# Seven-product down projection: when two activation sums are formed, where four result sums are kept, and how many pages the weight stream may use

## The chip, the cores and the metric

The kernel runs on one core of a Trainium2 chip. The metric is device time in microseconds, from a launch to its end. Its engines run side by side, each through its own queue in order: TensorE (PE, with its weight loads as PEld), VectorE (DVE), ScalarE (ACT), GpSimd (POOL), and SyncE (SP), which here only issues DMAs.

## What is computed

A two-layer decoder trunk over 256 tokens of width 2048, in float32. Each layer is a token mixer with an output projection, then a gated feed-forward block; each of the two adds a normed result to the stream x. The change lies in the feed-forward block and in the helpers it shares:

```
def swiglu(u, w_gu, w_down):
    gu = u @ w_gu                                            # (256, 2048) @ (2048, 2*5632)
    return (jax.nn.silu(gu[..., :D_FF]) * gu[..., D_FF:]) @ w_down   # (256, 5632) @ (5632, 2048)
x = x + rmsnorm(swiglu(rmsnorm(x, g[2]), ...), g[3])
```

## The kernel before, in words

**Products.** Float32 accuracy comes from splitting each operand into a rounded part and a remainder (hi, lo) and adding three matmuls: hi·hi, lo·hi, hi·lo. Activations are split once; weights are streamed and split as they come.

**Pages.** SBUF is cut into 44 pages of 4 KB per partition (`NPAGE`, class `Pages`), handed out first freed, first used. A page may be handed out while the engines still have to read it in the order of the queues; the new writer then waits for that reader.

**The weight stream.** `_unit_list` writes down the order of all weight units (128x1024, 512 KB). `dma_one` loads one into a page (a raw unit); `split_one` makes hi on ScalarE (L231) and lo on VectorE (L232), two pages, and gives the raw page back. `take` (L270 on) is called once for each unit: it returns the unit's parts and, before that, works ahead: twice it loads until 3 raw units are held and splits one further unit, then it loads a fourth raw unit (L284). `room(n)` lets it do so only while n pages beyond `st["res"]` (the reserve) are free; `st["look"]` bounds how many units ahead may be split. With no page to spare a unit is split only at its own `take`. `give` hands the two pages back behind the unit's last matmul.

**Side work.** Evacuations, norms and sums are generators; `tick`, called between matmul groups, advances one of them by one step, and a yielded number is the count of ticks to its next step. So side work is queued on ScalarE and VectorE between splits, in the order of the calls.

**Feed-forward.** `ffn` first runs the gate-up stage: 22 groups of 256 columns, each of 8 units (L928, `x_unit`, matmuls at L398 to L400). `gu_evac` turns a group into the transposed activations `hT` (one page per group, 22 in all), and for the last 8 groups (`DN_S`, 14 to 21) also into four sums of 128x128 blocks, `sp` (one page each, `s_parts`, L878, read from PSUM). The normed input `xf` takes 8 pages, released when the last `hT` page is claimed.

**Down projection.** `pair(cp)` runs twice, for the first and the last 1024 columns. For 14 of the 22 row groups it multiplies plainly (`x_step`: units of kind a and b, 12 matmuls each at L954 to L956). For the other 8 it uses a seven-product scheme on 2x2 blocks (`quad`: 4 takes named a, b, T13 and T24, 21 matmuls of 128x512; VectorE forms weight differences at L247, L248, L257 and L258). `_dn_steps` lays the kinds out: in pair 0 four a steps first, in pair 1 three, then the S steps woven among the others, and b steps last. All eight PSUM banks hold P1 to P7 and Q. After the last S step `sums` forms four combined sums in two pages of their own (`ut`, L988). `block` (L1004) then adds one result bank to its sum (VectorE, L1007), and `Tail.rows` squares it on ScalarE for the norm (L633) and multiplies it by the norm's gain row into a page `og` (VectorE, L639). The four blocks of pair 0 are queued while pair 1 runs its second unit. The gain rows `gb` come by a broadcast DMA from POOL's queue, which also carries the `xraw` loads of the next stage. In pair 1 each step frees one `hT` page and an S step also its `sp` page; x is read back into 4 pages, and layer 0 fills 8 pages `mT` and claims 8 pages `kT` for what follows, `mem_k`. The last four b units are taken together (`last_units`).

Of the kernel before, what the change touches and what calls it, by code (L numbers as in the profile page):

```python
# [10 lines left out]
F32 = mybir.dt.float32  # L11
F32R = mybir.dt.float32r
BF16 = mybir.dt.bfloat16
AF = mybir.ActivationFunctionType
OP = mybir.AluOpType
AX = mybir.AxisListType

P = 128
S = 256
D = 2048  # L20
KT = D // P
HD = 128
DFF = 5632
FT = DFF // P
# [69 lines left out]

DN_S = tuple(range(14, FT // 2))


def _dn_steps(cp):  # L100
# [93 lines left out]
def trunk(ctx: ExitStack, tc: tile.TileContext, a: dict, out: bass.AP):  # L194
    nc = tc.nc
    sb = ctx.enter_context(tc.tile_pool(name="sb", bufs=1))
    tmp = ctx.enter_context(tc.tile_pool(name="tmp", bufs=1))
# [9 lines left out]
    raws, parts = {}, {}  # L207
# [59 lines left out]
    def room(n):  # L267
        return len(pages.own) + len(pages.free) >= st["res"] + n

    def take(name):  # L270

        i = st["i"]
        assert units[i][0] == name, (units[i], name)
        while st["dma"] <= i:
            dma_one()
        while st["split"] <= i:
            split_one()
        n = len(units)
        for _ in range(0 if st["quiet"] else 2):
            while st["dma"] < n and len(raws) < NRAW and room(1):  # L280
                dma_one()
            if st["split"] < min(i + 1 + st["look"], n, st["dma"] - 1 if st["dma"] < n else n) and room(2):
                split_one()
        while not st["quiet"] and st["dma"] < n and len(raws) < 4 and room(1):  # L284
            dma_one()
        st["i"] += 1
        return parts.pop(i)
# [9 lines left out]
    def spawn(g):  # L297
        side.append([g, clock["t"]])
# [28 lines left out]
    def need(X, kts):  # L327
        until(lambda: X.done.issuperset(kts))
# [73 lines left out]
    def x_unit(pts, name, X, kt0, w, first, last, free=False):  # L402

        u = take(name)
        for k in range(2):
            need(X, (kt0 + k,))
            for t in range(2):
                x_mm(pts[t][1], u, X, kt0 + k, k, t, w, first and k == 0, last and k == 1)
                tick()
                tick()  # L410
        give(u)
        if free:
            X.drop()
# [203 lines left out]
    class Tail:  # L617
# [14 lines left out]
        def rows(self, c, t, src, pre=None):  # L632
            nc.scalar.activation(junk[:, :512], src, AF.Square, accum_out=self.ssq[:, t, c:c + 1])  # L633
            if pre is not None:
                rstd_of(pre, self.ssq[:, t, c:c + 1], t, self.r)
            hs, pg = slice((c % 2) * 512, (c % 2 + 1) * 512), 2 * t + c // 2
            if pg not in self.og:
                self.og[pg] = pages.get([P, 1024], F32, "og")
            nc.vector.tensor_tensor(out=self.og[pg][1][:, hs], in0=src, in1=self.gb[c // 2][1][:, hs], op=OP.mult)  # L639
            if c == 1 and t == 1:  # L640
                pages.put(self.gb.pop(0)[0])

        def chunk(self, c, pts, ts=(0, 1), pre=None):
            self.gain((c + 1) // 2 if c < 3 else 1)
            for t in ts:
                self.rows(c, t, pts[t][1], pre)
                banks.put(pts[t][0])
# [227 lines left out]
    free_mem(0)  # L875


    def s_parts(A):  # L878

        sv = tmp.tile([P, 4, P], F32, tag="sv", name="sv")  # L880
        sp = pages.get([P, 4, 2, P], F32R, "sp")
        tt = nc.vector.tensor_tensor
        s1 = tmp.tile([P, P], F32, tag="s11", name="s11")
        nc.scalar.activation(s1, A[:, 0, 1], AF.Copy)
        tt(out=sv[:, 0], in0=A[:, 1, 1], in1=s1, op=OP.add)
        tt(out=sv[:, 1], in0=sv[:, 0], in1=A[:, 0, 0], op=OP.subtract)
        tt(out=sv[:, 2], in0=A[:, 0, 0], in1=s1, op=OP.subtract)
        tt(out=sv[:, 3], in0=A[:, 1, 0], in1=sv[:, 1], op=OP.subtract)
        yield 1
        nc.scalar.activation(sp[1][:, :, 0, :], sv, AF.Copy)  # L890
        nc.vector.tensor_tensor(out=sp[1][:, :, 1, :], in0=sv, in1=sp[1][:, :, 0, :].bitcast(F32), op=OP.subtract)
        return sp

    def gu_evac(f2, pts, H, rf, Sp):

        while "r" not in rf:
            yield 0
        H.grow()
        hs = []
        for t in range(2):  # L900
            r = rf["r"][:, t:t + 1]
            g = tmp.tile([P, S], F32, tag="ev1", name="ev1", bufs=2)
            nc.scalar.activation(g, pts[t][1][:, :S], AF.Silu, scale=r)  # L903
            h = tmp.tile([P, S], F32, tag="ev2", name="ev2", bufs=2)
            nc.vector.scalar_tensor_tensor(h, pts[t][1][:, S:], r, g, op0=OP.mult, op1=OP.mult)  # L905
            banks.put(pts[t][0])
            hs.append(h)
        yield 8
        (b, p), = yield from sbank()
        for k in range(2):  # L910
            for t in range(2):
                nc.tensor.transpose(p[:, k * S + t * P:k * S + (t + 1) * P], hs[t][:, k * P:(k + 1) * P], ident)
        pv = p.rearrange("p (k q) -> p k q", k=2)
        hp = H.t[f2][1]
        yield 2
        nc.scalar.activation(hp[:, :, 0, :], pv, AF.Copy)
        nc.vector.tensor_tensor(out=hp[:, :, 1, :], in0=pv, in1=hp[:, :, 0, :].bitcast(F32), op=OP.subtract)
        if f2 in DN_S:
            Sp[f2] = yield from s_parts(p.rearrange("p (k t q) -> p k t q", k=2, t=2))
        banks.put(b)  # L920
        H.done.update((2 * f2, 2 * f2 + 1))

    def ffn(l, X, rf, gidx, step=lambda u: None, first=lambda c: None):
        H, Sp = XT(pages, 0, "hT"), {}
        st["res"] = 2
        for fs in [(0, 1)] + [(f2,) for f2 in range(2, FT // 2)]:
            pts = [[bank(), bank()] for _ in fs]
            for u in range(KT // 2):  # L928
                for p in pts:
                    x_unit(p, f"gu{l}", X, 2 * u, 512, u == 0, u == KT // 2 - 1)  # L930
            for f2, p in zip(fs, pts):
                spawn(gu_evac(f2, p, H, rf, Sp))
        until(lambda: len(H.t) == FT // 2)
        X.release()
        st["res"] = 3
        tail = Tail(gidx, "f")
        steps = 0

        def pair(cp):
            bk, n, T = {}, {}, {}  # L940
# [44 lines left out]
            def sums():  # L985

                yield 12
                tp = [pages.get([P, 2, 512], F32, "ut") for _ in range(2)]  # L988
                s1, u2, u3, v = (tp[j // 2][1][:, j % 2, :] for j in range(4))
                T["pages"], T["left"] = tp, 4  # L990
                tt = nc.vector.tensor_tensor
                nc.scalar.activation(s1, bk["P1"][1], AF.Copy)
                free("P1")
                tt(out=u2, in0=bk["P6"][1], in1=s1, op=OP.add)
                free("P6")
                tt(out=u3, in0=bk["P7"][1], in1=u2, op=OP.add)
                free("P7")
                yield 2
                tt(out=v, in0=bk["P5"][1], in1=u3, op=OP.add)
                tt(out=u2, in0=bk["P5"][1], in1=u2, op=OP.add)  # L1000
                free("P5")
                T["c"] = {"P2": (0, 0, s1), "P3": (1, 0, u2), "P4": (0, 1, u3), "Q": (1, 1, v)}

            def block(key, pre=None):  # L1004

                c, t, s_ = T["c"][key]
                nc.vector.tensor_tensor(out=s_, in0=bk[key][1], in1=s_, op=OP.add)  # L1007
                free(key)
                tail.rows(2 * cp + c, t, s_, pre)
                T["left"] -= 1  # L1010
                if not T["left"]:
                    for e in T["pages"]:
                        pages.put(e[0])

            def blocks_of(keys):
                yield 8
# [43 lines left out]
            body = plan if cp == 0 else plan[:-HOLD]  # L1060
            for j, (kd, u) in enumerate(body):
                if kd == "S":
                    need(H, (2 * u, 2 * u + 1))
                    until(lambda: u in Sp)
                    quad(u)
                    if cp == 1:
                        pages.put(Sp.pop(u)[0])
                        H.drop_one(u)
                else:
                    x_step(kd, u)  # L1070
                    if cp == 1 and kd == "b":
                        H.drop_one(u)
                if cp == 1 and kd in "Sb":
                    on_step()
                left = [e[0] for e in plan[j + 1:]]
                if "S" not in left and kd == "S":
                    spawn(sums())
                if "a" not in left and "S" not in left and (kd == "a" or kd == "S") and cp == 1:
                    spawn(blocks_of(("P2", "P4")))
            if cp == 0:  # L1080
                tail.gain(1)
                spawn(blocks_of(("P2", "P3", "P4", "Q")))
            else:
                last_units(plan[-HOLD:])
# [2 lines left out]
        pair(1)  # L1087
        tail.finish()
        H.release()
        return tail  # L1090

    Xf = XT(pages, KT, "xf")
# [409 lines left out]
```

## Time and profile before

| | |
|---|---|
| median of 3 runs | 2570.41 us (2570.28 to 2574.23) |
| the profiled execution | 2570.08 us, its span 2568.3 us |
| DVE, ACT, POOL busy | 1623.4, 1257.5, 59.9 us |
| DMA | 491.26 MB, mean 191 GB/s |
| layer 0: gate-up ends, pair 1 starts, down projection ends | about 1123, 1242 and 1364 us |
| layer 1: the same | about 2325, 2442 and 2558 us |

The span runs from the first to the last instruction. A matmul lasts longer in the records than the distance to the next one, since they are pipelined; so the pace is read from starts, or from how many matmuls a stretch holds. "Idle" is the time an engine had nothing running before an instruction, put down to what came last.

### The profile page before, as it was taken

The numbers are of one execution on the slowest core, as the hardware profiler recorded it, in microseconds if no ns is written. First come the engines' busy times: TensorE is split into PE (matmuls) and PEld (weight loads), VectorE is DVE, ScalarE is ACT, GpSimd is POOL, SyncE is SP. The second block draws the span as 40 slices with busy tenths as digits, with TensorE's granted clock in tenths as the row PEclk, the third lists the DMA queues.
The fourth block names the chain that finished last, engine by engine and source line by source line (L and its number), as shares of the span: only waits on it lengthen the run. The fifth ranks groups of instructions, "written<-read, shape, count | busy, mean of one in ns | idle before, by whom it ended". The sixth has DMA issues, their size and how long they took to land. (4 is left out here: it accounts for less than half of the span.)

```text
span 2568.3 us, 32470 instructions
## 1 busy us (share of the span) xinstructions
PE 2512.2 (98%) x12230; PEld 2121.7 (83%) x12230; DVE 1623.4 (63%) x2230; ACT 1257.5 (49%) x1804; POOL 59.9 (2%) x73
## 2 busy tenths in 40 slices
PE   8999999999999999999999999999899999999998
PEld 6899999988888888878787888888788888877876
DVE  8564555567544455568797766796644555547796
ACT  7444444456433344444565566565543444445553
POOL 5000000000000000000000000000000000000000
PEclk9999999999999999999999999999999999999999
DMA  8455555576555555556575676346655555546664
GB/s 304 147 182 170 170 161 177 173 256 245 188 185 184 181 180 167 162 180 209 190 271 203 213 243 212 115 140 222 202 175 182 182 183 174 165 148 213 205 217 176
DMA packets 138318, 491.26 MB, mean 191 GB/s; under 512 B 15664, under 2 KB 15664, under 8 KB 138160
## 3 DMA queue, kind: packets, MB, share of 16 engines
q1 hardware_dynamic: 134208, 477.06, 57.0%
q0 software_dynamic: 3232, 11.01, 1.3%
q8 instruction: 96, 1.57, 0.3%
q10 hardware_dynamic: 720, 1.11, 0.1%
q14 instruction: 62, 0.51, 0.1%
HBM read 482.82 MB, written 6.29 MB: 190 GB/s over the span
## 5 line engine op out<-in xcount | busy, mean ns | idle before, releaser
L232 DVE TENSOR_TENSOR lo<-raw,hi 128x1024 fp32r<-128x1024 f32 (+2 forms) x899 | 1048.7, 1205 | 360.7 <-ACT hi L231 327.9
L231 ACT ACTIVATE hi<-raw 128x1024 fp32r<-128x1024 f32 (+2 forms) x899 | 891.7, 1036 | 237.3 <-PE bk L400 131.6
L398 PE MATMUL bk<-hi,xf 128*128 128x512 f32 x1408 | 554.9, 394 | 5.3 <-ACT hi L231 4.7
L400 PE MATMUL bk<-lo,xf 128*128 128x512 f32 x1408 | 550.4, 391 | 1.5 <-DVE lo L232 1.4
L399 PE MATMUL bk<-hi,xf 128*128 128x512 f32 x1408 | 549.4, 390 | 0.0
L363 PE MATMUL bk<-xT,hi 128*128 128x512 f32 x1104 | 398.7, 404 | 0.0
L398 PEld LDWEIGHTS bk<-hi,xf 128*128 128x128 f32 x1408 | 265.6, 189 | 59.5 <-ACT hi L231 5.6
L400 PEld LDWEIGHTS bk<-lo,xf 128*128 128x128 f32 x1408 | 265.3, 188 | 59.2 <-DVE lo L232 3.5
L399 PEld LDWEIGHTS bk<-hi,xf 128*128 128x128 f32 x1408 | 265.7, 189 | 53.7 <-DVE xf L452 0.2
L365 PE MATMUL bk<-xT,lo 128*128 128x256 f32 x1035 | 289.5, 280 | 0.0
L363 PEld LDWEIGHTS bk<-xT,hi 128*128 128x128 f32 x1104 | 204.0, 188 | 39.8 <-issue 0.2
L954 PE MATMUL bk<-hi,hT 128*128 128x512 f32 x544 | 213.5, 392 | 6.4 <-ACT hi L231 6.4
L956 PE MATMUL bk<-lo,hT 128*128 128x512 f32 x544 | 213.6, 393 | 2.4 <-DVE lo L232 2.4
L955 PE MATMUL bk<-hi,hT 128*128 128x512 f32 x544 | 212.7, 391 | 0.0
L365 PEld LDWEIGHTS bk<-xT,lo 128*128 128x128 f32 x1035 | 195.4, 189 | 3.1
L905 DVE SCALAR_TENSOR_TENSOR ev<-bk,r_f,ev 128x256 f32<-128x256 f32 x88 | 42.2, 484 | 202.1 <-ACT ev L903 193.1
L903 ACT ACTIVATE ev<-bk,r_f 128x256 f32<-128x256 f32 x88 | 41.5, 474 | 227.4 <-PE bk L400 226.3
L954 PEld LDWEIGHTS bk<-hi,hT 128*128 128x128 f32 x544 | 103.0, 189 | 29.2 <-ACT hi L231 8.1
L956 PEld LDWEIGHTS bk<-lo,hT 128*128 128x128 f32 x544 | 102.8, 189 | 25.9 <-DVE lo L232 4.6
L955 PEld LDWEIGHTS bk<-hi,hT 128*128 128x128 f32 x544 | 102.8, 189 | 21.3
L390 ACT ACTIVATE ev<-bk 128x256 f32<-128x256 f32 x93 | 35.6, 383 | 129.5 <-PE bk L363 129.5
L391 DVE TENSOR_TENSOR ev<-bk,ev 128x256 f32<-128x256 f32 x93 | 39.3, 423 | 91.5 <-ACT ev L390 90.8
(246 smaller groups left out, 3037.6 us busy)
## 6 DMA issues: line engine op xcount, KB each, us to landing
raw<-in_gu SPq DMA_DIRECT2D x352, 512.0 KB, 3.6
raw<-in_dn SPq DMA_DIRECT2D x176, 512.0 KB, 4.4
raw<-in_a_qk SPq DMA_DIRECT2D x96, 512.0 KB, 3.8
raw<-in_a_v SPq DMA_DIRECT2D x64, 384.0 KB, 3.1
raw<-in_cw SPq DMA_DIRECT2D x32, 512.0 KB, 4.6
raw<-in_b_out SPq DMA_DIRECT2D x32, 512.0 KB, 4.2
raw<-in_a_out SPq DMA_DIRECT2D x24, 512.0 KB, 4.4
raw<-in_b_q SPq DMA_DIRECT2D x24, 512.0 KB, 3.9
```

Source lines behind the costliest of these rows:

```text
L231: nc.scalar.activation(hi, src, AF.Copy)
L232: nc.vector.tensor_tensor(out=lo, in0=src, in1=hi.bitcast(F32), op=OP.subtract)
L363: mm(pt[:, :], lhsT=hi[:, ks], rhs=X.hl(kt), start=first, stop=last)
L365: mm(pt[:, S:], lhsT=lo[:, ks], rhs=X.part(kt, 0), start=False, stop=False)
L398: mm(p[:, :w], lhsT=xh, rhs=u[0][1][:, ws], start=f, stop=False)
L399: mm(p[:, :w], lhsT=xl, rhs=u[0][1][:, ws], start=False, stop=False)
L400: mm(p[:, :w], lhsT=xh, rhs=u[1][1][:, ws], start=False, stop=l)
L903: nc.scalar.activation(g, pts[t][1][:, :S], AF.Silu, scale=r)
L905: nc.vector.scalar_tensor_tensor(h, pts[t][1][:, S:], r, g, op0=OP.mult, op1=OP.mult)
L954: mm(p, lhsT=xh, rhs=wh, start=f, stop=False)
L955: mm(p, lhsT=xl, rhs=wh, start=False, stop=False)
L956: mm(p, lhsT=xh, rhs=wl, start=False, stop=e)
```

## The change

- The same 8 row groups take the seven-product scheme, in another order: 14, 15, 16, 17, 20, 21, 18, 19. For 18 and 19 (`DN_LATE`) the block sums are no longer formed in the gate-up stage. A new generator `s_late`, queued as the down projection starts, adds hi and lo of `hT` back together into a page `hw` (VectorE, 128x512) and forms the sums from there.
- `take` loads the fourth raw unit only with three pages to spare (`room(3)`).
- In the last gate-up group `x_unit` gives back one page of `xf` after each unit.
- `sums` writes its four sums into the halves of the `og` pages, waiting until two pages are free, and `Tail.rows` multiplies them there in place. The `ut` pages are gone.
- The second gain row is loaded when the first is given back.
- The reserve in the down projection is 2 or 0 by step, where it was 3; the bound of units split ahead is 6 there.

```
-DN_S = tuple(range(14, FT // 2))
+DN_S = (14, 15, 16, 17, 20, 21, 18, 19)
+DN_LATE = (18, 19)
...
-        while not st["quiet"] and st["dma"] < n and len(raws) < 4 and room(1):
+        while not st["quiet"] and st["dma"] < n and len(raws) < 4 and room(3):
...
             if c == 1 and t == 1:
                 pages.put(self.gb.pop(0)[0])
+                self.gain(1)
...
-            self.gain((c + 1) // 2 if c < 3 else 1)
...
+    def s_late(H, Sp):
+
+        for u in DN_LATE:
+            h = H.t[u][1].bitcast(F32)
+            i, w = pages.get([P, 2, S], F32, "hw")
+            nc.vector.tensor_tensor(out=w, in0=h[:, :, 0, :], in1=h[:, :, 1, :], op=OP.add)
+            A = w.rearrange("p k (t q) -> p k t q", t=2)
+            Sp[u] = yield from s_parts(A, A[:, 0, 1])
+            pages.put(i)
+            yield 16
...
-        if f2 in DN_S:
-            Sp[f2] = yield from s_parts(p.rearrange("p (k t q) -> p k t q", k=2, t=2))
+        if f2 in DN_S and f2 not in DN_LATE:
+            Sp[f2] = yield from s_psum(p)
...
-                    x_unit(p, f"gu{l}", X, 2 * u, 512, u == 0, u == KT // 2 - 1)
+                    x_unit(p, f"gu{l}", X, 2 * u, 512, u == 0, u == KT // 2 - 1, fs[0] == FT // 2 - 1)
...
-        st["res"] = 3
...
+        spawn(s_late(H, Sp))
...
                 yield 12
-                tp = [pages.get([P, 2, 512], F32, "ut") for _ in range(2)]
-                s1, u2, u3, v = (tp[j // 2][1][:, j % 2, :] for j in range(4))
-                T["pages"], T["left"] = tp, 4
+                while len(pages.free) + len(pages.own) < 2:
+                    yield 0
+                for t in range(2):
+                    tail.og[2 * t + cp] = pages.get([P, 1024], F32, "og")
+                st["res"] = 0
+                s1, u2, u3, v = (tail.og[2 * (j // 2) + cp][1][:, j % 2 * 512:(j % 2 + 1) * 512] for j in range(4))
...
                 if kd == "S":
+                    st["res"], st["look"] = 0 if j > 8 or cp else 2, 6
...
                 if "S" not in left and kd == "S":
+                    st["res"] = 2 if cp == 0 else 0
                     spawn(sums())
...
             if cp == 0:
-                tail.gain(1)
                 spawn(blocks_of(("P2", "P3", "P4", "Q")))
...
         H.release()
+        st["look"] = 4
```

## Rows read from the trace of the kernel before

**Rows 1.** The page, part 1: busy time of each engine over the span.
```profile
PE 2512.2 (98%) x12230; PEld 2121.7 (83%) x12230; DVE 1623.4 (63%) x2230; ACT 1257.5 (49%) x1804; POOL 59.9 (2%) x73
```

**Rows 2.** Waits of PE, whole span: who <- for whom: us, times, longest.
```profile
PE bk L398 <- ACT hi L231: 10.7, 3, 6.0
...
PE bk L954 <- ACT hi L231: 6.7, 5, 2.9
```

**Rows 3.** Waits of PE, layer 0, 1094 to 1128 us.
```profile
PE bk L398 <- ACT hi L231: 2.4, 1, 2.4
PE bk L954 <- ACT hi L231: 1.5, 1, 1.5
PE bk L400 <- DVE lo L232: 0.5, 1, 0.5
PE bk L956 <- DVE lo L232: 0.5, 1, 0.5
```

**Rows 4.** Timeline of PE, layer 1: start, us, instruction, [idle before].
```profile
2306.21 0.73 PE L398 MATMUL bk<-hi,xf 128*128 128x512 f32 x1 [2.37 <-ACT hi L231]
...
2326.20 0.50 PE L954 MATMUL bk<-hi,hT 128*128 128x512 f32 x1 [1.51 <-ACT hi L231]
...
2327.46 0.50 PE L956 MATMUL bk<-lo,hT 128*128 128x512 f32 x1 [0.52 <-DVE lo L232]
```

**Rows 5.** Stretches: length; busy and count of PE, PEld, DVE, ACT, POOL; PEclk; DMA.
```profile
1094.00:1112.00 18.00, 15.10 (x62) 11.75 (x61) 8.23 (x12) 5.62 (x9) 0.00 (x0) 0.91 0.33 114
1120.00:1132.00 12.00, 9.96 (x39) 7.51 (x38) 6.55 (x8) 5.72 (x8) 0.58 (x1) 0.86 0.84 309
1160.00:1200.00 40.00, 40.00 (x178) 32.73 (x177) 32.62 (x38) 19.99 (x22) 0.00 (x0) 1.00 0.65 211
1246.00:1258.00 12.00, 8.55 (x29) 6.24 (x28) 7.20 (x9) 5.43 (x10) 0.00 (x0) 0.86 0.42 124
...
1290.00:1330.00 40.00, 40.00 (x178) 33.14 (x177) 39.54 (x48) 26.44 (x34) 2.14 (x4) 1.00 0.80 261
...
1366.00:1380.00 14.00, 12.70 (x67) 11.03 (x68) 10.96 (x16) 7.26 (x11) 0.80 (x1) 0.88 0.86 336
...
2300.00:2312.00 12.00, 9.53 (x36) 6.96 (x36) 4.81 (x8) 4.29 (x6) 0.00 (x0) 0.86 0.21 65
2322.00:2332.00 10.00, 7.97 (x36) 5.96 (x36) 6.79 (x8) 6.29 (x8) 0.48 (x1) 1.00 0.86 297
```

**Rows 6.** The page, part 6: loads of down-projection units, median us to landing.
```profile
raw<-in_dn SPq DMA_DIRECT2D x176, 512.0 KB, 4.4
```

**Rows 7.** Waits of PE, layer 0, 1364 to 1372 us.
```profile
PE bk L363 <- ACT hi L231: 2.5, 1, 2.5
PE bk L365 <- DVE lo L232: 0.8, 1, 0.8
```

**Rows 8.** Waits of PE, layer 0, 1246 to 1268 us.
```profile
PE bk L954 <- ACT hi L231: 3.2, 2, 2.9
PE bk L956 <- DVE lo L232: 1.5, 3, 0.7
```

**Rows 9.** Waits of PE, layer 1, 2448 to 2460 us.
```profile
PE bk L956 <- DVE lo L232: 1.0, 2, 0.5
PE bk L954 <- ACT hi L231: 0.4, 1, 0.4
```

**Rows 10.** Timeline of DVE around 1245 us: start, us, instruction, [idle before].
```profile
1245.73 0.69 DVE L639 TENSOR_TENSOR og<-ut,gb 128x512 f32<-128x512 f32 x1
...
1256.35 0.69 DVE L232 TENSOR_TENSOR hl<-raw,hl 128x512 fp32r<-128x512 f32 x1 [2.64 <-ACT hl L231]
1258.21 0.69 DVE L247 TENSOR_TENSOR t<-raw,raw 128x512 f32<-128x512 f32 x1 [1.18 <-PE bk L955]
```

**Rows 11.** Timeline of ACT around 1247 us.
```profile
1247.12 0.63 ACT L633 ACTIVATE junk<-ut 128x512 bf16<-128x512 f32 x1 [0.60 <-DVE ut L1007]
```

**Rows 12.** DVE by line: the first of the four 128x128 block sums.
```profile
L885 DVE TENSOR_TENSOR sv<-sk,s 128x128 f32<-128x128 f32 x16 | 4.7, 292 | 5.5 <-ACT s L884 5.5
```

More of the change, by code (lines that the diff above doesn't have):

```diff
@@ L875, in trunk, with s_parts @@
     free_mem(0)
-    def s_parts(A):
+    def s_parts(A, a21):
         sv = tmp.tile([P, 4, P], F32, tag="sv", name="sv")
@@ L882, in s_parts @@
         tt = nc.vector.tensor_tensor
-        s1 = tmp.tile([P, P], F32, tag="s11", name="s11")
-        nc.scalar.activation(s1, A[:, 0, 1], AF.Copy)
-        tt(out=sv[:, 0], in0=A[:, 1, 1], in1=s1, op=OP.add)
+        tt(out=sv[:, 0], in0=A[:, 1, 1], in1=a21, op=OP.add)
         tt(out=sv[:, 1], in0=sv[:, 0], in1=A[:, 0, 0], op=OP.subtract)
-        tt(out=sv[:, 2], in0=A[:, 0, 0], in1=s1, op=OP.subtract)
+        tt(out=sv[:, 2], in0=A[:, 0, 0], in1=a21, op=OP.subtract)
         tt(out=sv[:, 3], in0=A[:, 1, 0], in1=sv[:, 1], op=OP.subtract)
@@ L892, in s_parts, with s_psum @@
         return sp
+    def s_psum(p):
+        A = p.rearrange("p (k t q) -> p k t q", k=2, t=2)
+        a21 = tmp.tile([P, P], F32, tag="s11", name="s11")
+        nc.scalar.activation(a21, A[:, 0, 1], AF.Copy)
+        return (yield from s_parts(A, a21))
+    def s_late(H, Sp):
[7 more added lines that the diff above has]
+            yield 16
     def gu_evac(f2, pts, H, rf, Sp):
@@ L1009, in block @@
                 tail.rows(2 * cp + c, t, s_, pre)
[L1010 to L1013, printed above, removed]
             def blocks_of(keys):
```

## The prediction

> **What bounds the kernel.** First the page's busy times: TensorE is busy 98% of the span, VectorE 63% [rows 1]. The change adds and removes no matmul, since the same eight row groups take the seven-product form; so it can move the time only through the moments at which TensorE stands still or runs slowly. Next, the waits of TensorE: nearly all of those on weights are waits for a split, ScalarE's hi or VectorE's lo (L398 on ACT hi 10.7 us, L954 on ACT hi 6.7) [rows 2]. Then I asked where they lie. Three kinds of place hold them, and all three border on the down projection.
>
> **Place 1, gate-up into down projection.** Layer 0 idles 2.4 + 1.5 + 0.5 + 0.5 = 4.9 us in four waits [rows 3], layer 1 2.37 + 1.51 + 0.52 = 4.4 us in three [rows 4]. Two costs come on top. A matmul lasts 0.39 us in the records but the next starts 0.23 later (40.00 us hold 178, with one or two across the edges [rows 5]), so each wait delays the start by 0.16 us more than its idle time. And after some waits the granted clock falls to 1.2 GHz: 0.91 over 18 us and 0.86 over 12 us in layer 0, 0.86 over 12 us in layer 1 [rows 5]. What a fall costs is the missing share times the stretch: 0.09 x 18 = 1.6 us, 0.14 x 12 = 1.7 us. Layer 0: 4.9 + 4 x 0.16 + 1.6 + 1.7 = 8.8 us. Layer 1: 4.4 + 0.5 + 1.7 = 6.6 us. Together **15.4 us**.
>
> The cause is pages, counted from the code. At the third unit of the last gate-up group live pages are xf 8, hT 21, sp 7, and in layer 0 one with the memory values: 37 of 44. Seven are left, two of them reserved: three raw units and one pair of split parts. So a unit is split at its own take, behind the evacuation of the group before; and the first down-projection units are split behind the last group's evacuation.
>
> After the change two sp pages are missing there (groups 18 and 19) and two xf pages have come back by the third unit: 11 are left instead of 7, so three raws and three pairs. At the border all eight xf pages are back: 17. Three units of lead are 3 x 12 x 0.227 = 8.2 us of matmuls, more than any of these waits. I take all 15.4 us as gained. Bounds: nothing, if the order of the queues and not the pages holds the split back; above, the 15.4. It is nearer the whole, because the shortage is in the code's own count.
>
> The fourth raw unit that now needs three pages is costed at nothing: a load lands in 4.4 us [rows 6], and three raws cover 8.2 us of TensorE. Without that cover a late load would cost up to 4.4 us per unit. The page order makes it unlikely.
>
> **Place 2, the end of layer 0's down projection.** TensorE idles 2.5 + 0.8 us on the first mem_k unit [rows 7], and the clock then is 0.88 over 14 us, 1.7 us [rows 5]: 3.3 + 2 x 0.16 + 1.7 = 5.3 us. The unit is split only after the last blocks, for lack of pages: 32 live, four held pairs, reserve 3. After the change the two ut pages and the reserve are free, 14 pages for the stream: four held pairs, three raws and one pair, so the first mem_k unit is ready. The second is still split behind the last squares; its lo comes some 0.9 us late by the same chain. I take **4.2 us** gained (bounds 0 and 5.3).
>
> **Place 3, pair 0 into pair 1.** Here the four blocks of pair 0 sit in VectorE's and ScalarE's queues ahead of the splits. Layer 0: 3.2 + 1.5 us in five waits [rows 8] and a clock of 0.86 over 12 us [rows 5], 4.7 + 0.8 + 1.7 = 7.2 us. Layer 1: 1.4 us in three waits [rows 9], 1.9 us.
>
> The in-place product makes this chain longer. Now VectorE runs add, product, add, product at 0.69 us each [rows 10], while ScalarE squares beside it in 0.63 us [rows 11]. After the change the product overwrites what the square reads, so it waits for it, and the next block's add is queued behind the product: 0.69 + 0.63 + 0.69 and two short hand-overs, some 2.1 us a block instead of 1.35. Four blocks: **3.1 us** more. Behind them wait ScalarE's and VectorE's splits for the first S step, which need 4 x 0.69 us for weight differences as well, and for those TensorE.
>
> Against it stands a deeper lead. ut is gone and the reserve is 0: ten pages (layer 1 eleven) serve the stream, two to three pairs ahead, where today it is often none. In layer 0 that removes two page stalls of VectorE, 2.64 + 1.18 = 3.8 us [rows 10], so 7.2 becomes about 6.5. In layer 1 no such stall stands today; one lo of 1.2 us is done earlier, but the blocks now stand behind a split that waits about 2 us longer for its page. I set lateness 1.9 + 3.1 - 1.2 + 0.8 (half of a clock fall of 1.7) = 4.6. Sum for place 3: 11.1 against 9.1 today, **2.0 us lost**; bounds: all 9.1 gained if the lead hides the chain, or 2 x 3.1 + 2 x 1.7 = 9.6 lost if the lead gives nothing.
>
> Here a rule bears on the clock. Equal idle of 1.5 us at the start of the down projection is followed by a fall in layer 0 (0.86) and by none in layer 1 (1.00) [rows 5]. The Trainium skill, "TensorE: Matmul & The Clock Gate", section "What's actually happening", says that the activity monitor's window runs freely, so where a gap falls in it matters, not its length alone; the rows agree. By that rule the new layer-1 wait costs 0 or 1.7 us of clock and never the 0.8 that I enter, and the sum would come out 0.8 us lower or 0.9 higher.
>
> **Moved or added at no cost.** The late sums: per row group one 128x512 add more on VectorE (0.69) plus four ops of 0.29 [rows 12] and a split, all at the start of pair 0, where VectorE is busy 32.6 us of 40 [rows 5] and the lead is full; ScalarE loses a small copy. If that cover went they would cost up to 2 x 0.7 us per layer. The group order 20, 21 before 18, 19 gives them time. The second gain row's DMA moves behind the fourth block; its reader is 80 us away, and the xraw loads behind it on POOL's queue today wait for pages anyway: nothing, at worst one load's 4.4 us hidden by step distance. In the out projections it moves within two column chunks. The last block after each down projection keeps its order: there VectorE's scalar op for the norm already waits for the square ahead of the product.
>
> **The sum.** -15.4 - 4.2 + 2.0 = -17.6 us against the profiled execution's 2570.08, 2552.5; the median lies 0.3 us above that execution: **2552.8 us**.
>
> **Rivals.**
> *All stalls go* (0.20). The deeper lead hides the longer chain: 15.4 + 5.3 + 9.1 = 29.8 us, 2540.6. For it: all these waits come from splits that are late by under 3 us, one unit's matmuls. Against: the splits of the first S step share VectorE with the chain.
> *Slower through VectorE in pair 1* (0.05). In layer 0 VectorE is busy 39.54 of 40 us there [rows 5], so whatever it loses TensorE loses. With reserve 0, the stream and the mT, kT and x pages take pages just handed back. If each of the eight S steps had one page stall as now seen once, 1.18 us [rows 10], that is 9.4 per layer, 18.9, and with 2 x 3.1 for the products 25.1 against 19.6 gained: 2575.9. It decides once VectorE loses over 9.8 us per layer. Against: much of its work there fills the lead.
> *The change does not do what it says* (0.08). The splits at place 1 are late because ScalarE works in order behind the evacuation, whatever the pages: then -4.2 + 2.0, 2568.2, no change. Against: a unit already split needs nothing more from ScalarE.
>
> **Chances and range.** My forecast 0.62, rivals 0.20, 0.05, 0.08, and 0.05 for anything else. A measurement here can tell 0.2%, 5.1 us. The forecast and the first rival lie below 2565.3 except where half of place 1 stays and place 3 loses its 9.6: I give that 0.02 to "same". Faster 0.84, same 0.10, slower 0.06. The range reaches from all stalls gone (2540.6, less 1.6 for one more clock fall) to a forecast with half of place 1 lost (2552.8 + 7.7, and 2.5 more at place 3): 2539 to 2563.
>
> **What would show it.** Right: no wait on ACT hi at the gate-up border, granted clock 1.00 there; mem_k's first wait under 1 us; L639's product starting after L633's square, blocks about 2.1 us apart, and waits of 4 to 7 us in all at each pair border. Wrong: the waits of rows 3 and 4 still there; no wait at the pair border; or new waits on lo spread over pair 1 with VectorE idle on pages.

## The result, and the profile after

The changed kernel takes 2595.84 us (median of 4 runs, 2594.73 to 2596.64), the kernel before 2570.35 us beside it: ratio 1.0097, 95% interval 1.0079 to 1.0114. It is 25.5 us **slower**; 2552.8 us were forecast. The count of matmuls is the same, and their idle time is not. (Lines below the change move: L231 and L232 are now L232 and L233, L954 to L956 are L971 to L973, L633, L639 and L1007 are L634, L640 and L1027.)

The page, part 1, of the changed kernel, beside [rows 1]:

```profile
PE 2523.7 (97%) x12230; PEld 2116.8 (82%) x12230; DVE 1628.3 (63%) x2234; ACT 1257.8 (48%) x1800; POOL 57.7 (2%) x73
```

VectorE and ScalarE do nearly the work they did. The waits of TensorE over the whole span of the changed kernel (who <- for whom: us, times, longest), beside [rows 2]:

```profile
PE bk L973 <- DVE lo L233: 18.2, 32, 1.4
PE bk L971 <- ACT hi L232: 9.1, 10, 4.1
PE bk L364 <- ACT hi L232: 7.8, 1, 7.8
...
PE bk L399 <- ACT hi L232: 5.6, 1, 5.6
```

The last one is the kernel's start. Of L399's three waits before, the two at the gate-up borders are gone. But the down projection now waits 32 times for VectorE's lo, where in the kernel before it waited 7 times:

```profile
PE bk L956 <- DVE lo L232: 3.6, 7, 0.7
```

Stretches of the changed kernel show where (columns as in [rows 5]):

```profile
1094.00:1112.00 18.00, 18.00 (x83) 14.89 (x82) 11.98 (x16) 9.95 (x12) 0.00 (x0) 1.00 0.70 229
...
1160.00:1200.00 40.00, 37.77 (x160) 29.24 (x159) 29.88 (x33) 17.86 (x19) 0.00 (x0) 1.00 0.50 167
1250.00:1262.00 12.00, 7.71 (x22) 4.74 (x20) 8.83 (x12) 4.30 (x10) 0.00 (x0) 0.75 0.18 64
1290.00:1330.00 40.00, 37.09 (x158) 28.88 (x157) 32.26 (x37) 19.99 (x23) 0.54 (x1) 1.00 0.51 174
1376.00:1390.00 14.00, 5.78 (x27) 4.39 (x26) 10.04 (x18) 6.06 (x13) 1.80 (x2) 0.72 0.39 137
2300.00:2312.00 12.00, 12.00 (x54) 9.94 (x53) 5.83 (x5) 4.41 (x5) 0.00 (x0) 1.00 0.69 212
```

The gate-up borders (1094 and 2300 us) are full, with the clock at 2.4 GHz throughout. Yet 1160 to 1200 us in pair 0 holds 160 matmuls where 178 ran before, and 1290 to 1330 us in pair 1 holds 158. VectorE is *less* busy there, 32.26 of 40 us against 39.54 [rows 5]. So it is no bound: it is itself waiting.

What the two splitting engines wait for tells why. The waits of ScalarE in the kernel before, layer 1, second half of pair 0 (2385 to 2441 us):

```profile
ACT hi L231 <- PE bk L955: 16.9, 8, 3.9
ACT hi L231 <- PE bk L956: 6.6, 3, 2.4
ACT hi L231 <- DVE lo L232: 4.2, 6, 1.4
```

and of the changed kernel at the same place (2400 to 2456 us):

```profile
ACT hi L232 <- DVE lo L233: 15.7, 12, 1.3
ACT hi L232 <- DVE t L249: 8.1, 3, 2.8
ACT hi L232 <- DMA raw<-in_dn: 4.5, 3, 2.4
```

Before, ScalarE waited here mostly for TensorE, so it was ahead. Now it waits for VectorE, the last reader of the page that hi is to be written to, and a little for loads. VectorE in turn needs that hi (12.2 us of waits for it in this stretch before, 15.1 us now). Two engines that ran side by side take turns. In layer 0 (1180 to 1240 us) of the changed kernel the loads weigh as much:

```profile
ACT hi L232 <- DVE lo L233: 11.0, 7, 2.6
ACT hi L232 <- DMA raw<-in_dn: 8.8, 3, 4.4
ACT hl L232 <- DMA raw<-in_dn: 7.1, 3, 3.5
ACT hi L232 <- DVE t L249: 6.4, 3, 2.3
```

The same stretch of layer 0 before has no wait on a load. Yet ScalarE's longest wait there was for VectorE too, for a weight difference that it needs as input, and TensorE waited for nothing in these 60 us:

```profile
ACT hi L231 <- DVE raw L258: 18.5, 4, 4.6
...
ACT hi L231 <- DVE lo L232: 1.3, 1, 1.3
```

So a wait of ScalarE for VectorE does not cost time by itself; what the changed kernel adds is the waits on lo and on loads.

Where the time went, from the starts of the first matmuls in the timelines. A pair has 504 matmuls, which at 0.227 us from start to start, without a wait, take 114.4 us; "between" runs from the last matmul of layer 0's down projection to the first of layer 1's.

| us | start to pair 0 | pair 0 | pair 1 | between | pair 0 | pair 1 | tail |
|---|---|---|---|---|---|---|---|
| before | 1124.4 | 117.3 | 121.9 | 962.6 | 115.6 | 116.4 | 10.1 |
| changed | 1116.1 | 125.1 | 135.5 | 958.3 | 123.1 | 125.7 | 10.1 |
| difference | -8.3 | +7.8 | +13.6 | -4.3 | +7.5 | +9.3 | 0 |

The border gains came (in "between" a new loss at mem_k hides part of layer 1's). The four pairs together lost more.

### The profile page after: what moved, and what is told of

Its sections match the earlier page's. It is cut to its first block, busy times and chain, and to the rows that moved or that the text cites. A ratio compares the mean times of both kernels' runs of the same rounds, so it can differ in the third digit from the quotient of the medians.

```text
span 2593.8 us, 32432 instructions
## 1 busy us (share of the span) xinstructions
PE 2523.7 (97%) x12230; PEld 2116.8 (82%) x12230; DVE 1628.3 (63%) x2234; ACT 1257.8 (48%) x1800; POOL 57.7 (2%) x73
## 4 chain that ended last, share of the span: by engine, by line
PE 81%; DVE 10%; ACT 4%; issue 3%; DMA 2%; POOL 0%; SPq 0%; DVEq 0%; ACTq 0%; POOLq 0%
PE bk L400 16%; PE bk L401 16%; PE bk L399 16%; PE bk L364 12%; PE bk L366 6%; DVE lo L233 5%; PE bk L973 3%; ACT hi L232 3%; PE bk L971 3%; PE bk L972 3%; DMA raw<-in_dn 1%; PE sk L928 1%; PE sk L569 1%; PE bk L1205 1%; PE bk L1204 1%
## 5 line engine op out<-in xcount | busy, mean ns | idle before, releaser
L233 DVE TENSOR_TENSOR lo<-raw,hi 128x1024 fp32r<-128x1024 f32 (+2 forms) x899 | 1055.1, 1206 | 411.5 <-ACT hi L232 367.8
L232 ACT ACTIVATE hi<-raw 128x1024 fp32r<-128x1024 f32 (+2 forms) x899 | 896.2, 1037 | 286.0 <-DVE lo L233 84.3
L399 PE MATMUL bk<-hi,xf 128*128 128x512 f32 x1408 | 552.9, 393 | 0.6 <-ACT xf L452 0.6
L399 PEld LDWEIGHTS bk<-hi,xf 128*128 128x128 f32 x1408 | 264.7, 188 | 53.7 <-ACT xf L452 0.8
L973 PE MATMUL bk<-lo,hT 128*128 128x512 f32 x544 | 213.9, 393 | 5.3 <-DVE lo L233 5.3
L971 PE MATMUL bk<-hi,hT 128*128 128x512 f32 x544 | 214.2, 394 | 4.7 <-ACT hi L232 4.7
L972 PE MATMUL bk<-hi,hT 128*128 128x512 f32 x544 | 212.6, 391 | 0.0
L973 PEld LDWEIGHTS bk<-lo,hT 128*128 128x128 f32 x544 | 102.5, 188 | 32.2 <-DVE lo L233 10.6
L971 PEld LDWEIGHTS bk<-hi,hT 128*128 128x128 f32 x544 | 102.7, 189 | 27.6 <-ACT hi L232 7.9
L972 PEld LDWEIGHTS bk<-hi,hT 128*128 128x128 f32 x544 | 102.7, 189 | 21.2
```

The source lines that it names most:

```text
L232: nc.scalar.activation(hi, src, AF.Copy)
L233: nc.vector.tensor_tensor(out=lo, in0=src, in1=hi.bitcast(F32), op=OP.subtract)
L399: mm(p[:, :w], lhsT=xh, rhs=u[0][1][:, ws], start=f, stop=False)
L971: mm(p, lhsT=xh, rhs=wh, start=f, stop=False)
L972: mm(p, lhsT=xl, rhs=wh, start=False, stop=False)
L973: mm(p, lhsT=xh, rhs=wl, start=False, stop=e)
```

## The experiments

Twelve kernels, each timed beside the kernel before; the ratio is to that one.

| what differs | us | ratio, 95% interval |
|---|---|---|
| changed, reserve 3 | 2551.46 | 0.9926 (0.9911 to 0.9941) |
| changed, fourth raw unit with one page to spare | 2568.07 | 0.9989 (0.9980 to 0.9998) |
| changed, 4 units ahead | 2581.28 | 1.0041 (1.0026 to 1.0055) |
| before, border parts alone | 2553.26 | 0.9933 (0.9919 to 0.9948) |
| before, youngest page first | 2656.90 | 1.0334 (1.0319 to 1.0350) |
| changed, reserve 2 | 2556.05 | 0.9942 (0.9925 to 0.9959) |
| changed, reserve 3 and fourth raw unit | 2556.07 | 0.9944 (0.9929 to 0.9959) |
| changed, reserve 3, product deferred | 2542.99 | 0.9894 (0.9879 to 0.9909) |
| the same, reserve 4 | 2542.73 | 0.9892 (0.9876 to 0.9909) |
| the same, reserve 3, at the end 0 | 2541.63 | 0.9888 (0.9873 to 0.9902) |
| changed, product deferred | 2589.09 | 1.0071 (1.0056 to 1.0086) |
| changed, splits need three pages | 2569.10 | 0.9993 (0.9983 to 1.0003) |

**The reserve.**

```
-                    st["res"], st["look"] = 0 if j > 8 or cp else 2, 6
+                    st["res"], st["look"] = 3, 6
...
-                    st["res"] = 2 if cp == 0 else 0
+                    st["res"] = 3
...
-                st["res"] = 0
+                st["res"] = 3
```

> The changed kernel with the reserve at 3 all through the down projection, everything else as changed. Theory R (reserve: with none, every page that a load, a hi or a lo is written to has only just been handed back, so loads and ScalarE wait for the last reader): the waits of TensorE on VectorE lo in the second half of pair 0 and in pair 1 (some 20 us with what hangs on them) go, the gain at the gate-up border stays: 2550 to 2560 us. Theory I (in-place product: the longer chain of blocks is what costs): nothing changes ahead of pair 1, 2585 to 2597 us. Theory F (fourth raw unit): still no fourth unit for lack of three spare pages, 2590 to 2600 us.

2551.46 us: three numbers alone turn 1% slower into 0.7% faster. The pairs take 116.6, 120.5, 114.9 and 117.6 us. ScalarE's waits in layer 1, second half of pair 0 (2365 to 2421 us):

```profile
ACT hi L232 <- PE bk L973: 6.3, 10, 1.7
ACT hi L232 <- PE bk L972: 5.1, 2, 2.8
ACT hi L232 <- DVE t L249: 4.0, 2, 2.0
ACT hl L232 <- DMA raw<-in_dn: 3.6, 3, 1.4
ACT hi L232 <- DVE lo L233: 3.5, 2, 1.8
ACT hi L232 <- DMA raw<-in_dn: 2.6, 2, 1.3
```

It waits mostly for TensorE again, and 3.5 us for lo instead of 15.7. Its waits on loads, 6.2 us, are no shorter than the changed kernel's 4.5 here, and pair 0 takes 114.9 us with them: in this stretch the loads were not the loss. Theory R holds; I falls as the main cause, and F is not needed to explain this gain.

**The fourth raw unit.**

```
-        while not st["quiet"] and st["dma"] < n and len(raws) < 4 and room(3):
+        while not st["quiet"] and st["dma"] < n and len(raws) < 4 and room(1):
```

> The changed kernel with the fourth raw unit loaded again with one page to spare. Theory F (three raws instead of four make loads late): back to 2550 to 2570 us, ScalarE's waits on loads in pair 0 gone. Theory R: a fourth raw unit only takes one more of the few pages, the free list gets shorter still: 2590 to 2605 us.

2568.07 us: this gives back 27.8 us of the 44.4, with the reserve at 0. Here R's expectation was wrong and F's right. So either the earlier load matters by itself, or the fourth raw unit keeps a page from the splits; the last experiment was meant to separate the two.

**Units ahead.**

```
-                    st["res"], st["look"] = 0 if j > 8 or cp else 2, 6
+                    st["res"], st["look"] = 0 if j > 8 or cp else 2, 4
```

> The changed kernel with at most 4 units split ahead in the down projection, as before, instead of 6. Theory R: in pair 0 only 3 to 4 units are split ahead anyway, so it stays there; in the second half of pair 1 more pages stay free: 2585 to 2596 us. A theory that the deeper split eats the pages of the loads: 2560 to 2575 us.

2581.28 us, below what R expected and above the other theory. Pair 0 stays as bad (124.9 and 124.0 us), pair 1 recovers some (129.5 and 123.1) and so does the border to mem_k: fewer split units leave pages lying, where enough are split. This reason was not tested further.

**The border parts alone.** The kernel before with `DN_LATE`, the new order and `s_late`, and

```
-                    x_unit(p, f"gu{l}", X, 2 * u, 512, u == 0, u == KT // 2 - 1)
+                    x_unit(p, f"gu{l}", X, 2 * u, 512, u == 0, u == KT // 2 - 1, fs[0] == FT // 2 - 1)
```

> The kernel before with only the parts that act at the gate-up border: sums of groups 18 and 19 formed late, their order, xf pages handed back unit by unit. No change of reserve, raw units, result sums or gain row. All theories but one: the waits there go, 2570.4 - 15.4 = 2555 us (2551 to 2560). If instead the late sums cost what the border gives: 2565 to 2575 us.

2553.26 us, 17.3 us gained; no wait of TensorE is left between 1094 and 1128 us. In layer 0 the late sums seem to cost something, right behind them. VectorE runs the last of them until 1129 us, and between 1128 and 1140 us TensorE waits (L972 and L974 here are L971 and L973 of the changed kernel):

```profile
PE bk L974 <- DVE lo L233: 0.7, 1, 0.7
PE bk L972 <- ACT hi L232: 0.4, 1, 0.4
```

47 matmuls run in these 12 us, where 55 ran before. The changed kernel has two waits there as well (0.7 and 0.7 us). That the sums cause them is read from the order of VectorE's queue; no run tests it. Pair 0 takes 116.6 and 114.9 us all the same, 0.7 less than before in each layer, because the waits at its start are gone.

**Age of a page.** If a reserve helps because it leaves pages lying until their readers are done, then handing out the same pages in the other order must hurt with every count as it was:

```
-        i = (first or second).pop(0)
+        i = (first or second).pop(-1 if stream and self.young else 0)
...
+        pages.young = True
         pair(0)
         pair(1)
+        pages.young = False
```

> The kernel before, reserve 3 and all counts of pages unchanged; in the down projection a load or a split part takes the page that was handed back last, not the one that was handed back first. Theory R in its sharper form (what the reserve buys is the age of a page: with three pages always lying free, the page written next was handed back long ago): ScalarE's hi waits for VectorE's lo and loads wait for their page as in the changed kernel, 2580 to 2610 us. If the reserve only mattered by how many units are split ahead, which this edit does not touch: 2568 to 2573 us.

2656.90 us, more than either theory said: 86 us for an order, with reserve 3, four raw units, and as many units split ahead in the queues' order as before. Waits of TensorE over the span:

```profile
PE bk L954 <- ACT hi L231: 36.4, 23, 3.4
PE bk L956 <- DVE lo L232: 20.0, 34, 0.7
```

and of ScalarE in layer 0's pair 0 (1200 to 1260 us):

```profile
ACT hl L231 <- PE bk L956: 15.5, 4, 4.4
ACT hi L231 <- DVE t L248: 8.1, 4, 2.0
ACT hi L231 <- PE bk L956: 6.2, 6, 1.2
ACT hi L231 <- DVE lo L232: 5.2, 4, 1.3
```

The second and fourth line are the changed kernel's. The others name TensorE, as before the change, but here they do not mean that ScalarE is ahead: it waits for the page of the unit that TensorE is just using, while TensorE runs short. So the order alone, with every count unchanged, can cost this much; the reader that is waited for is mostly another one than in the changed kernel.

**Reserve 2**, at all three places:

> The changed kernel with a reserve of 2 all through the down projection. Theory R: most of the gain of reserve 3 (2551.5 us), with some waits on VectorE lo left in pair 1: 2552 to 2565 us. If any reserve under 3 loses it all: 2580 to 2597 us.

2556.05 us: most of the gain, with pair 1 at 125.4 and 119.3 us.

**Reserve 3 and the fourth raw unit**, the first two edits together:

> Reserve 3 as in the first experiment, and the fourth raw unit again with one page to spare. Theory R: with a reserve the fourth unit hardly matters, 2549 to 2555 us. Theory F by itself (the fourth unit is worth some 28 us whatever the reserve): below 2535 us.

2556.07 us, by the medians 4.6 more than with three raws. Once pages lie free, the fourth raw unit gains nothing. It lies just above the range of R and far from F's.

**The product deferred**, on top of reserve 3. `Tail.rows` returns the product as a function, and `block` queues it behind the next add:

```
                 free(key)
-                tail.rows(2 * cp + c, t, s_, pre)
+                flush()
+                p = tail.rows(2 * cp + c, t, s_, pre, pre is None)
+                if p:
+                    held.append(p)
```

> Reserve 3 as in the first experiment; the gain product of a block is queued behind the next block's add, so that VectorE no longer stands still for ScalarE's square. If the in-place product is what keeps 6.5 and 3.6 us of lost TensorE time at the pair borders: blocks 1.35 to 1.5 us apart instead of 2.1 and 2 to 6 us gained on 2551.5, 2545.5 to 2549.5 us. If the page and split order is what binds there: 2550 to 2553 us.

2542.99 us, 8.5 below reserve 3 alone and 2.5 below the range that I expected. VectorE's timeline in the changed kernel (start, us, instruction, [idle before]):

```profile
1246.57 0.68 DVE L1027 TENSOR_TENSOR og<-bk,og 128x512 f32<-128x512 f32 x1
1248.04 0.69 DVE L640 TENSOR_TENSOR og<-og,gb 128x512 f32<-128x512 f32 x1 [0.79 <-ACT junk L634]
1248.65 0.68 DVE L1027 TENSOR_TENSOR og<-bk,og 128x512 f32<-128x512 f32 x1
1250.18 0.69 DVE L640 TENSOR_TENSOR og<-og,gb 128x512 f32<-128x512 f32 x1 [0.85 <-ACT junk L634]
```

and in this experiment:

```profile
1234.48 1.28 DVE L1039 TENSOR_TENSOR og<-bk,og 128x512 f32<-128x512 f32 x2
1235.95 0.69 DVE L642 TENSOR_TENSOR og<-og,gb 128x512 f32<-128x512 f32 x1 [0.19 <-ACT junk L634]
1236.56 0.68 DVE L1039 TENSOR_TENSOR og<-bk,og 128x512 f32<-128x512 f32 x1
1237.16 0.68 DVE L642 TENSOR_TENSOR og<-og,gb 128x512 f32<-128x512 f32 x1
1237.76 0.68 DVE L1039 TENSOR_TENSOR og<-bk,og 128x512 f32<-128x512 f32 x1
```

Adds stand 2.1 us apart with the in-place wait; without it four start within 3.3 us, 1.1 apart on average. Pair 1 falls to 116.2 and 114.6 us, near its 114.4.

**Reserve 4**, with the product deferred:

> Reserve 4 with the product queued behind the next add, where reserve 3 gave 2543.0 us. Theory R: the age of a page is enough at 3, a fourth reserved page only shortens the lead: 2541 to 2550 us. If age still binds at 3: 2535 to 2540 us.

2542.73 us, the same: three pages are enough.

**Reserve 0 at the very end**, with the product deferred:

```
                 drain()
+                st["res"] = 0
                 us = [take(f"dn{l}") for _ in range(HOLD)]
```

> Reserve 3 with the deferred product, and reserve 0 from the moment the last four units of a down projection are taken together. My step on the border to mem_k: the first mem_k unit is then split early and TensorE's wait of 2.5 us there goes, 2538 to 2540.5 us. If the pages then are too young: 2542 to 2548 us.

2541.63 us, the fastest of all by its median, and between the two ranges expected. The intervals of this and of the two before overlap, so they count as equal. TensorE's waits between 1345 and 1360 us:

```profile
PE sk L696 <- DVE x L685: 0.7, 1, 0.7
PE bk L366 <- DVE lo L233: 0.6, 1, 0.6
```

The first mem_k unit is ready, as my second step had it, and 2.5 us of waiting are gone; with reserve 3 kept they stand there unchanged. "Between" is 2.7 us shorter for it, but pair 1 of layer 0 1.0 us longer; by the medians the whole gains 1.4 us, which is not clear of noise.

**The changed kernel with only the product deferred.**

> The changed kernel, its reserve of 0 as changed, with only the deferred product. The in-place product then costs what it cost with reserve 3, 8.5 us: 2584 to 2590 us. If with reserve 0 the product's wait is what tips pair 1 over: below 2575 us. If it is hidden under the waits for pages: 2592 to 2597 us.

2589.09 us: 6.8 us less than the changed kernel, near the 8.5 that it costs with reserve 3. The two losses nearly add up.

**One more page kept from the splits**, in the changed kernel:

```
-            if st["split"] < min(i + 1 + st["look"], n, st["dma"] - 1 if st["dma"] < n else n) and room(2):
+            if st["split"] < min(i + 1 + st["look"], n, st["dma"] - 1 if st["dma"] < n else n) and room(3):
```

> The changed kernel, reserve 0 and at most three raw units as changed; a unit is split ahead only with three pages to spare instead of two, so one page more lies free behind each split, and no load comes earlier by count. If what the fourth raw unit gave back (28 us) was a page kept from the splits, so that hi and lo go to older pages: 2560 to 2580 us. If it was the earlier load itself: 2588 to 2600 us.

2569.10 us: 26.7 us back, nearly as much as the fourth raw unit gave, by *splitting later*. TensorE's waits over the span:

```profile
PE bk L971 <- ACT hi L232: 8.4, 6, 4.0
PE bk L973 <- DVE lo L233: 8.1, 13, 0.7
```

18.2 us of waiting on lo are 8.1. The total is what the theory of older pages expected. But the gain does not lie where the fourth raw unit's lay: the pairs take 116.8, 131.8, 119.0 and 121.0 us here, and 119.9, 126.5, 114.9 and 120.3 there. And in layer 0's pair 0 (1178 to 1238 us), where TensorE waits for nothing any more, ScalarE does:

```profile
ACT hi L232 <- DVE lo L233: 18.9, 12, 2.8
ACT hi L232 <- DVE t L249: 7.9, 3, 2.6
ACT hi L232 <- PE bk L973: 2.6, 1, 2.6
ACT hi L232 <- DVE raw L259: 1.6, 4, 0.4
```

That is more waiting on lo than in the changed kernel (11.0 us) and none on a load (there 15.9 us). So loads did come earlier, against what was expected, and the experiment does not separate young pages under hi from late loads.

## Why the prediction was wrong

**The cause.** Pages are handed out first freed, first used, so the more of them lie free, the longer a page rests before it is written again. A reserve of 3 is not idle space that may be spent. With a reserve of 0 the planner splits ahead until, in pair 0, mostly two or three pages lie free as a `take` begins, by a count of the planner's own state, against five before. Then hi of the next unit goes to a page whose reader, VectorE's lo or a weight difference, has only just begun, and a load goes out late. Shown: reserve 3 alone brings 44.4 us back (2595.84 to 2551.46), reserve 2 39.8; a younger order of the same pages alone costs 86, with the lead in the queues untouched; keeping one page from the splits brings back 26.7.

Not shown is how the loss divides between hi on young pages and late loads. A count from the code says which pages hi gets in layer 0's pair 0 once the reserve is 0. Before, and with reserve 3, none of 42 was handed back as late as the `take` before; in the changed kernel 34 of 42 were, 12 of them by a split. With the fourth raw unit it is 40 of 42, but only 6 by a split, because the extra load takes those pages; with the three-page rule it is 25 of 43, 19 by a split. (With the fourth raw unit mostly two pages lie free there as a `take` begins, in the changed kernel mostly three.) So the two partial remedies work by different routes, and the time follows neither the number of free pages nor the age of hi's page alone.

**The step that failed** is in place 3: "Against it stands a deeper lead. ut is gone and the reserve is 0: ten pages (layer 1 eleven) serve the stream, two to three pairs ahead, where today it is often none." I counted the three reserved pages as gained for splitting. The lead came, by the same count: in pair 0 mostly two or three units are split ahead as a `take` begins, where it was none or one. But the pages were worth more lying free. The forecast put 2.0 us of loss on both pair borders; the four pairs lost 7.8 + 13.6 + 7.5 + 9.3 = 38.2 us, and not at the borders alone: the loss starts inside pair 0, in layer 0 at about 1180 us, behind the step that sets the reserve to 0, where I had seen nothing. The sign of being wrong that came true is the last one named, new waits on lo, spread wider than pair 1.

**A second step failed with it:** "The fourth raw unit that now needs three pages is costed at nothing ... The page order makes it unlikely." With reserve 0 giving it up cost 27.8 us. Late loads, which I named as the price, do stand in the trace (15.9 us of ScalarE's waits in layer 0's stretch above), beside hi written to pages that a split had just handed back; which weighs more is open. With reserve 3 giving it up costs nothing.

**Place 1 was right.** 15.4 us forecast. The border parts alone gained 17.3 by the medians and 15.5 between the two traces: layer 0 reaches its down projection 7.4 us sooner, "between" is 6.6 shorter, and pair 0 is 0.7 us shorter in each layer. My reading that the pages, and not the order of the queues, held the splits back is borne out: the waits of [rows 3] and [rows 4] are gone. The late sums, put at nothing, stand in front of two new waits of 1.1 us in layer 0, within the bound of 2 x 0.7 us that I gave them.

**Place 2 was wrong in the changed kernel.** 4.2 us of gain were forecast. TensorE's waits from 1376 to 1392 us, against 3.3 us in [rows 7]:

```profile
PE bk L364 <- ACT hi L232: 7.8, 1, 7.8
PE bk L366 <- DVE lo L233: 0.5, 1, 0.5
```

The first mem_k unit was split early, as I said, and ran; the wait is the second one's. It is queued behind the last blocks, and these were late. ScalarE's first copy for the sums of pair 1:

```profile
1372.12 0.58 ACT L1012 ACTIVATE og<-bk 128x512 f32<-128x512 f32 x1
```

That is 4.5 us ahead of the projection's last matmul (its start at 1376.66); before it was 24 us ahead, at 1339.6. `sums` waits for two free pages while the stream takes them all: by the count of the planner it runs six units after it is queued, where it was two. The prediction has no term for this wait.

**Place 3, the in-place product, was right in kind and near in size.** I priced 0.75 us a block, 6.2 us for two chains, and 0.8 for half a clock fall. The adds do stand 2.1 us apart. Deferring the product gains 8.5 us with reserve 3, 6.8 with 0; part of it may be more than the change had added, since adds now stand closer (1.1 us) than the 1.35 of before.

**The rivals.** "Slower through VectorE in pair 1" named the mechanism, pages just handed back, and the sign, and had 0.05. It failed on two points. I held VectorE to be the bound, by its 39.54 busy us of 40 [rows 5], and so counted only its own page waits; in fact that busy time was filling a lead, ScalarE and the loads wait for pages as well, and VectorE ended less busy. And I placed it in pair 1 alone. "All stalls go" forecast 2540.6, and the fastest kernel here takes 2541.6. That is no proof of this rival: it let a deeper lead hide the longer chain, and that kernel keeps the reserve nearly to the end and shortens the chain.

The changed kernel with a reserve of 3 takes 2551.5 us, near the forecast of 2552.8. The agreement is partly luck. The 4.2 us of place 2 are not in it: the first mem_k waits of 2.5 and 0.8 us stand as before. Nor is the 2.0 us loss of place 3: pair 1 takes 120.5 and 117.6 us against 121.9 and 116.4. What carries the miss is the reserve, together with the fourth raw unit that became dear with it.

## What to carry to other kernels

In a pool that hands out the longest-freed buffer, a buffer lying free is a wait avoided: count a reserve as distance between the last reader and the next writer, and before spending it look at what the producers wait for. If they wait for each other where they used to wait for the consumer, the pool may have run too young. It is a warning and no proof: ScalarE waited 18.5 us for VectorE in a stretch of the kernel before, and 18.9 us for lo in one of the last experiment, while TensorE waited for nothing. Only the consumer's own waits tell what it costs. An in-place step across two engines also makes a wait; queue the next independent step ahead of it.

## What was not expected of the hardware

Waits too short to stand out add up without the clock showing them. From 1160 to 1200 us the changed kernel's TensorE did 160 matmuls against 178 while its granted clock stayed at 1.00, 2.4 GHz; between 1180 and 1250 us eight waits on lo make 4.5 us and none is longer than 0.7. Around the one wait of 4.1 us in 1250 to 1262 us the clock was 0.75.
